# Each link between ScalarE and VectorE half a step later, in an encoder block with seven-product projections

## The chip, the cores and the metric

The kernel runs on one core of one Trainium2 chip. The time is the device time of an execution in microseconds. The core's engines are TensorE (PE in the profile: matmuls; PEld: its weight loads), VectorE (DVE), ScalarE (ACT), GpSimd (POOL) and SyncE (SP). Each has a queue that it works off strictly in the order in which the program issued, waiting on semaphores where an operand is not ready. DMAs are issued from SP, ACT or POOL.

## The reference

One layer of a hybrid encoder block on x (256 tokens, 2048 wide), all float32:

```python
xn = rms_norm(x, norm_pre_w)
u_lru, g_lru, q, k, v, g_attn, m_lru, m_attn = split(xn @ w_in)       # 2048 x 13312
u = centred_depthwise_conv(u_lru, conv_w, conv_b)
h = rg_lru(u, forward) + rg_lru(u, reverse)       # gates by 16 blocks of 128x128
y_a = h * silu(g_lru)
y_b = windowed_gqa(rope(q), rope(k), v, sink) * silu(g_attn)          # 16 heads, 4 kv heads
merged = sigmoid(m_lru) * (y_a @ w_proj_a) + sigmoid(m_attn) * (y_b @ w_proj_b)
out = x + rms_norm(merged @ w_out, norm_post_w)
```

## The kernel before

**Split products.** Every float32 operand is split into a high part (rounded to fp32r by a ScalarE cast) and a low part (what the cast left, by a VectorE subtraction). A product is then three fp32r matmuls: high by high, high by low, low by high (`mm3`, L226 to L228; in the wide form of a block, L249 and L250). So for each weight block ScalarE makes `wh` (L221) and VectorE makes `wl` (L223), both 128x1024 halves. `parts_of` (L152) does the same for activations: a cast (L153), then a subtraction (L154).

**Steps.** The program is a list of steps, each with a 1 MB block of weights; a step has two half-steps, each with 1024 columns of it. `load_plan` writes the order: 164 steps, 328 half-steps. A step is a "blk" (128 output columns in transposed form), a "quad" (a quarter of K for 512 columns, 12 matmuls of 512 in a half-step) or a "part" (one of the seven products, 6 matmuls of 512 in a half-step). The stages in order: u; the projections for the LRU branch and both SiLU gates (`gl`, `ga`, `u`); k and v; q with heads and the `ml` and `pa` products between; the merge gate of the attention branch (`ma`, `am`); four `pb` products; the output (`o`, `om`).

**The order within a half-step** is the loop at the end of `body`. At half-step hs it issues the loads (SP's queue; `fetch` with a lead of three steps, into three `raw` buffers), then everything registered for hs with `at` or `soon`, then `split(hs + 4)`, then what is registered `behind` hs, then the half-step's matmuls:

```python
for fn in due.pop(hs, ()):
    fn()
if hs >= FIRST:
    split(hs + 4)
```

So the cast of wh and the subtraction of wl stand next to each other in time, four half-steps ahead of their matmuls; there are five buffers for each. `soon(fn, d)` registers for d half-steps later. Within a function that is called at one half-step, a chain that goes from ScalarE to VectorE or back is issued whole: copy, add, scale, sigmoid, multiply in `silu_evac` and `scaled` (L523 to L528, L665, L666), reduce, exponentials in `expo`, cast and subtract in `parts_of`.

**Seven products.** Half of the merge gate (columns 512 to 1023 and so on, as named in `GATE`) and half of the output are computed in Strassen's manner: seven products of half size on sums of quarters, in place of eight. The sums of activations are made per 256 rows of K: `sums_of_parts` adds the parts of xs (`xx..a`, L319), `sums_of` makes four sums from it (`xx..f`, L311 to L313), and half a step later `parts_of` splits them into `xx`. Eight such calls are registered behind half-steps 3, 5, ... 17 of the gate. For the output the sums come from the transposed merged values (`turn`, L831; `mx`). The sums of weights are made by DMA: a cell (`amx0a` and so on: x or y, quarter 0 or 1, half a or b) is loaded, and after the product that used it, another block is added into it by a DMA from POOL's queue (L188). m5, m6 and m4 follow one another in the x cells, m7 follows m3 in the y cells. An add cannot be issued before the cell's wh and wl have been made. The order of the gate's 22 steps (a digit first is a quad of a plain column):

```python
GATE = "2.0 2.1 2.2 2.3 m1.0 m1.1 m2.0 m2.1 3.0 m5.0 m5.1 m3.0 m3.1 3.1 m6.0 m6.1 m7.0 m7.1 3.2 m4.0 m4.1 3.3".split()
```

The products are combined after m2, m6, m7 and m4 (`after`; VectorE, L382 to L388, then `combine`, L857), and the combination goes to ScalarE: a sigmoid in the gate (L676), squares in the output (L911).

Of the kernel before, what the change touches and what calls it, by code (L numbers as in the profile page):

```python
# [35 lines left out]
FIRST = 8  # L36
# [87 lines left out]
def body(ctx, tc, x, xT, wall, wlru, pvec, npost, ident_d, mask_d, rope_d, out):  # L124
    nc = tc.nc
# [16 lines left out]
    def half_unit(name, tag, dt=F32, bufs=2):  # L142
        return small.tile([P, 2, S], dt, tag=tag, name=name, bufs=bufs)
# [5 lines left out]
    def tiny(name, n=2):  # L149
        return small.tile([P, n], F32, tag="tiny", name=name, bufs=24)  # L150

    def parts_of(h, l, src, cast=nc.scalar.copy):  # L152
        cast(h, src)  # L153
        nc.vector.tensor_tensor(l, src, h.bitcast(F32), ALU.subtract)  # L154

# [19 lines left out]
    def soon(fn, d=1):  # L175
        at(now[0] + d, fn)
# [121 lines left out]

    SUMS = ("s3", "s1", "s2", "s4")

    def sums_of(name, src, psum=True):
        a = src.rearrange("p a b -> p (a b)")
        a11, a12, a21 = (a[:, i * P:(i + 1) * P] for i in (0, 2, 1))
        f = half_unit(f"{name}f", "uu", F32).rearrange("p a (b c) -> p (a b) c", b=2)
        t = unit(name, F32R, (P, 4, 2, P))
        ends = src.rearrange("p a (b c) -> p (a b) c", b=2)[:, 0:4:3]
        if psum:

            nc.scalar.copy(f[:, 3], a21)
            a21 = f[:, 3]  # L310
        nc.vector.tensor_tensor(f[:, 0:2], ends, a21.unsqueeze(1).to_broadcast([P, 2, P]), ALU.subtract)  # L311
        nc.vector.scalar_tensor_tensor(f[:, 2], f[:, 1], -1.0, a11, ALU.mult, ALU.subtract)
        nc.vector.scalar_tensor_tensor(f[:, 3], f[:, 2], -1.0, a12, ALU.mult, ALU.subtract)  # L313
        return t, f

    def sums_of_parts(name, pair, sums):

        a = half_unit(f"{name}a", "uu", F32)
        nc.vector.tensor_tensor(a, pair[:, :, 0].bitcast(F32), pair[:, :, 1].bitcast(F32), ALU.add)  # L319
        t, f = sums_of(name, a, False)  # L320
        sums.append(t)
        soon(lambda: parts_of(t[:, :, 0], t[:, :, 1], f))

    class Seven:

# [194 lines left out]
        upads[n] = t  # L520
        return t

    def scaled(dst, ps):  # L523
        if len(ps.shape) == 4:
            nc.scalar.copy(dst, ps[:, :, 1])
            nc.vector.tensor_tensor(dst, ps[:, :, 0], dst, ALU.add)
            ps = dst
        nc.vector.tensor_tensor(dst, ps, rbc.unsqueeze(1).to_broadcast([P, 2, S]), ALU.mult)  # L528

    def evac_quad(n):  # L530
        scaled(upad_tile(n)[:, :, 2:2 + S], ups[n // 2][:, :, 0])
# [126 lines left out]
    def silu_evac(units_list, n):  # L658
        def done(ps):
            if n % 4 == 0:  # L660
                units_list.append(unit(f"sg{n}"))
            dst = units_list[n // 4][:, n % 4:n % 4 + 2]
            sg = half_unit(f"sig{n}", "p")
            scaled(dst, ps)
            nc.scalar.activation(sg, dst, AF.Sigmoid)  # L665
            nc.vector.tensor_tensor(dst, dst, sg, ALU.mult)  # L666
        return done

    tm, sm, ms, msum = {}, {}, [], []
# [25 lines left out]
    def add_heads(name, then):  # L695

        v = {}

        def evac(n):
            def done(ps):  # L700
                v[n] = half_unit(f"{name}f{n}", "uu")
                scaled(v[n], ps)
                for d in range(4):
                    soon(lambda d=d: rotate(n, d), d + 1)
            return done

        def rotate(n, d):
            t = v[n]
            r = t[0:ROT]
            if d == 0:  # L710
                v["s"] = small.tile([ROT, 2, S], F32, tag="upad", name=f"{name}s{n}", bufs=2)
                nc.vector.stream_shuffle(v["s"], r, swap)
                nc.vector.tensor_tensor(r, r, rope[:, 0].unsqueeze(1).to_broadcast([ROT, 2, S]), ALU.mult)
            elif d == 1:
                s = v["s"]
                nc.vector.tensor_tensor(s, s, rope[:, 1].unsqueeze(1).to_broadcast([ROT, 2, S]), ALU.mult)
                nc.vector.tensor_tensor(r, r, s, ALU.add)
            elif d == 2:
                if n == 0:
                    v["h"], v["l"] = unit(f"{name}h", F32R), unit(f"{name}l", F32R)  # L720
                parts_of(v["h"][:, n:n + 2], v["l"][:, n:n + 2], t)
            elif n == 2:
                then(v["h"], v["l"])
                v.clear()

        for n in (0, 2):
            add_pair(f"{name}{n}", xs, evac(n))
# [4 lines left out]
    def v_evac(t, ps):  # L732
        if t == 0:
            kv["vh"], kv["vl"] = (unit(f"v{s}", F32R, (P, 2, 512)) for s in "hl")
        vh, vl = kv["vh"][:, t], kv["vl"][:, t]
        nc.scalar.activation(vh, ps, AF.Copy, scale=rtok[:, t:t + 1])
        nc.vector.scalar_tensor_tensor(vl, ps, rtok[:, t:t + 1], vh.bitcast(F32), ALU.mult, ALU.subtract)

    add_rows("v_ps", xs, v_evac)

    def head(hd, qh, ql, b):
        g, j = hd // 4, hd % 4
        sk = pv[:, PV_SINK + hd:PV_SINK + hd + 1]
        ts = [slice(t * P, (t + 1) * P) for t in range(2)]
        v = {}

        def scores():
            v["sc"] = bank(f"sc{hd}")
            for t in range(2):
                mm3(v["sc"][:, t], qh[:, j, ts[t]], ql[:, j, ts[t]], kv["kh"][:, g], kv["kl"][:, g], True, True)  # L750

        def expo():
            p = v["p"] = half_unit(f"p{hd}", "p")
            sc = v.pop("sc")
            m, nm, es = tiny(f"m{hd}"), tiny(f"nm{hd}"), tiny(f"es{hd}")
            dn = v["dn"] = tiny(f"dn{hd}")
            for t in range(2):
                nc.vector.tensor_tensor_reduce(p[:, t], sc[:, t], mask[:, t], P ** -0.5, sk, ALU.add, ALU.max, m[:, t:t + 1])
            nc.vector.tensor_scalar(nm, m, -1.0, None, ALU.mult)  # L759
            for t in range(2):  # L760
                nc.scalar.activation(p[:, t], p[:, t], AF.Exp, bias=nm[:, t:t + 1], accum_out=dn[:, t:t + 1])  # L761
            nc.scalar.activation(es, nm, AF.Exp, bias=sk)
            v["es"] = es

        def normalise():
            dn, rd = v["dn"], tiny(f"rd{hd}")
            nc.vector.tensor_tensor(dn, dn, v["es"], ALU.add)
            nc.vector.reciprocal(rd, dn)
            for t in range(2):
                nc.vector.tensor_scalar(v["p"][:, t], v["p"][:, t], rd[:, t:t + 1], None, ALU.mult)  # L770

        def flip():
            v["pt"] = bank(f"pt{hd}")
            for kt in range(2):
                for t in range(2):
                    nc.tensor.transpose(v["pt"][:, kt, ts[t]], v["p"][:, t, ts[kt]], ident)

        def p_parts():
            t = unit(f"ph{hd}", F32R, (P, 2, 2, S))
            v["h"], v["l"] = t[:, 0], t[:, 1]  # L780
            parts_of(v["h"], v["l"], v.pop("pt"))

        def values():
            v["o"] = bank(f"o{hd}")
            ks = slice(g * P, (g + 1) * P)
            for kt in range(2):
                mm3(v["o"][:, 0], kv["vh"][:, kt, ks], kv["vl"][:, kt, ks], v["h"][:, kt], v["l"][:, kt], kt == 0, kt == 1)

        def gate_out():
            y = sga[g][:, j]  # L790
            nc.vector.tensor_tensor(y, v["o"][:, 0], y, ALU.mult)
            v.clear()

        for d, fn in ((0, scores), (1, expo), (2, normalise), (4, flip), (5, p_parts), (7, values), (8, gate_out)):
            at(b + d, fn)

    def yb_parts(q):
# [18 lines left out]
    def add_pb(c):  # L816
# [8 lines left out]
        def turn(i):  # L825

            ps = bank(f"mt{c}{i}")
            for j in range(2):
                sl = slice((2 * i + j) * P, (2 * i + j + 1) * P)
                for t in range(2):  # L830
                    nc.tensor.transpose(ps[:, j, t * P:(t + 1) * P], sm[c][:, t, sl], ident)  # L831
            m = pair_unit(f"ms{2 * c + i}")
            ms.append(m)
            parts_of(m[:, :, 0], m[:, :, 1], ps)
            t, f = sums_of(f"mx{2 * c + i}", ps)
            parts_of(t[:, :, 0], t[:, :, 1], f)
            msum.append(t)

        add_rows(f"pb{c}_", yb, done)

# [14 lines left out]
    def combine(name, ps, other, sign):  # L855
        f = small.tile([P, 512], F32, tag="p", name=name, bufs=2)
        nc.vector.scalar_tensor_tensor(f, ps, float(sign), other, ALU.mult, ALU.add if sign > 0 else ALU.subtract)  # L857
        return f

    mid = []  # L860
    for m, c in MID:
        mid.append((add_pa, c // 512) if m == "w_proj_a" else (add_ml, (c - ML0) // 512))
# [5 lines left out]
        f(n)  # L868

    xsum = []  # L870
    seven = Seven("am", "w_in", MA0, xs, xsum, lambda t, c, ps, *a: gate_evac(sm, c)(t, combine(f"af{t}{c}", ps, *a)))
    b = 2 * len(steps)
    for q in range(2):
        at(b - 4 + 3 * q, lambda q=q, s=seven: s.start("x", q))
# [54 lines left out]
                eng = nc.sync if q % 2 == 0 else nc.scalar  # L929
                eng.dma_start(out[t * P:(t + 1) * P, q * 512:(q + 1) * 512], y)  # L930

    seven = Seven("om", "w_out", 0, ms, msum, lambda t, c, ps, *a: o_done(t, c, combine(f"of{t}{c}", ps, *a)))
    for q in range(2):
        at(b - 16 + 4 * q, lambda q=q, s=seven: s.start("x", q))
        at(b - 12 + 4 * q, lambda q=q, s=seven: s.second(q))
# [5 lines left out]
    for i, (_, half) in enumerate(steps):  # L941
        for h in range(2):
# [8 lines left out]
            for fn in due.pop(hs, ()):  # L951
                fn()
            if hs >= FIRST:
                split(hs + 4)
            if hs in last:
                last.pop(hs)()
            half(h, *parts.pop(hs))
# [72 lines left out]
```

## Time and profile before

| | |
|---|---|
| median of 3 runs | 926.21 us (924.91 to 926.62) |
| profiled execution, its own time | 925.56 us |
| its span, first to last instruction | 923.8 us |
| PE busy | 902.9 us (98%) |
| DVE busy | 716.5 us (78%) |
| ACT busy | 567.5 us (61%) |
| POOL busy | 29.4 us (3%) |
| HBM read | 186.10 MB, 204 GB/s over the span |
| granted TensorE clock, mean | 0.992 |

A row of a group or of a timeline has the line of the kernel, the engine, the operation, out<-in by the names in the program (buffer numbers left out), shapes, and the time; in brackets the idle time of that engine just before, and whose end ended it. In a timeline the first number is the start in us from the span's start and the second the time taken; "x2" merges neighbours. In the list of waits the numbers are us in total, times, and the longest. A PE matmul's time contains its drain, which overlaps the next one: starts, not durations, give the pace.

### The profile page before, as it was taken

Reading aid. Unit: us, or ns where it says so; the run is one execution under the profiler, and the core shown is the slowest. Engines: PE = TensorE matmul, PEld = TensorE weight load, DVE = VectorE, ACT = ScalarE, POOL = GpSimd, SP = SyncE. Lnnn points to the kernel's source line nnn. Section 1 sums busy time; section 2 is a strip of 40 time slices with the busy share of each in tenths; the row PEclk is TensorE's granted clock in tenths of the full one; section 3 lists DMA queues with packets and bytes.
Section 4 is the critical chain, followed back from the end, with each engine's and each line's share of the span. In section 5 each row is a group of like instructions: output and inputs, shape, how many; then the busy total and the mean of one; then the engine's idle time right before and its main releaser. Section 6 shows DMA issues by size and latency. Waiting matters only on the chain.

```text
span 923.8 us, 12335 instructions
## 1 busy us (share of the span) xinstructions
PE 902.9 (98%) x4742; PEld 769.7 (83%) x4742; DVE 716.5 (78%) x1010; ACT 567.5 (61%) x794; POOL 29.4 (3%) x55
## 2 busy tenths in 40 slices
PE   9999999999999999999999999999978999999996
PEld 8898888888888888888888888888756788888885
DVE  6976968696979889896877878556677867778786
ACT  7678585858497875955554454644446654445653
POOL 0000000000000000000000000001003000100210
PEclk9999999999999999999999999999989999999999
DMA  9765455446455454466445444559769674987992
GB/s 339 264 216 193 158 203 201 168 155 230 154 205 205 157 186 169 154 224 228 144 176 182 148 172 140 180 186 292 258 203 191 146 259 176 302 293 280 231 317 102
DMA packets 33372, 189.00 MB, mean 205 GB/s; under 512 B 3712, under 2 KB 4480, under 8 KB 15264
## 3 DMA queue, kind: packets, MB, share of 16 engines
q1 hardware_dynamic: 27840, 170.14, 51.5%
q0 software_dynamic: 4608, 16.78, 9.6%
q10 hardware_dynamic: 864, 1.29, 0.4%
q8 instruction: 37, 0.61, 0.3%
q14 instruction: 23, 0.19, 0.1%
HBM read 186.10 MB, written 2.10 MB: 204 GB/s over the span
## 4 chain that ended last, share of the span: by engine, by line
PE 86%; issue 7%; DMA 3%; POOL 1%; DVE 1%; ACT 0%; SPq 0%; DVEq 0%; ACTq 0%; POOLq 0%
PE ga L250 6%; PE q L250 6%; PE gl L250 6%; PE u L250 5%; PE ga L249 3%; PE q L249 3%; PE gl L249 3%; PE u L249 2%; PE u_ps L509 2%; PE k L250 2%; PE omm L226 1%; PE omm L227 1%; PE omm L228 1%; DMA amx1b<-wall_dram 1%; PE o L228 1%
## 5 line engine op out<-in xcount | busy, mean ns | idle before, releaser
L223 DVE TENSOR_TENSOR wl<-raw,wh 128x1024 fp32r<-128x1024 f32 (+1 forms) x290 | 348.1, 1213 | 130.8 <-ACT wh L221 129.9
L221 ACT CAST wh<-raw 128x1024 fp32r<-128x1024 f32 (+1 forms) x289 | 296.1, 1043 | 122.1 <-PE q L250 14.4
L250 PE MATMUL ga<-xs,wh 128*128 128x512 f32 x256 | 90.6, 398 | 0.0
L250 PE MATMUL q<-xs,wh 128*128 128x512 f32 x256 | 89.8, 396 | 0.0
L250 PE MATMUL gl<-xs,wh 128*128 128x512 f32 x224 | 79.3, 398 | 0.0
L250 PE MATMUL u<-xs,wh 128*128 128x512 f32 x192 | 68.0, 398 | 0.0
L249 PE MATMUL ga<-xs,wl 128*128 128x256 f32 x240 | 67.5, 281 | 0.0
L249 PE MATMUL q<-xs,wl 128*128 128x256 f32 x240 | 67.1, 280 | 0.0
L249 PE MATMUL gl<-xs,wl 128*128 128x256 f32 x210 | 59.0, 281 | 0.0
L250 PEld LDWEIGHTS ga<-xs,wh 128*128 128x128 f32 x256 | 47.6, 188 | 10.4
L250 PEld LDWEIGHTS q<-xs,wh 128*128 128x128 f32 x256 | 47.4, 188 | 9.9
L249 PE MATMUL u<-xs,wl 128*128 128x256 f32 x180 | 50.6, 281 | 0.0
L250 PEld LDWEIGHTS gl<-xs,wh 128*128 128x128 f32 x224 | 41.7, 188 | 9.1
L249 PEld LDWEIGHTS ga<-xs,wl 128*128 128x128 f32 x240 | 45.4, 189 | 0.6
L249 PEld LDWEIGHTS q<-xs,wl 128*128 128x128 f32 x240 | 45.3, 189 | 0.7
L250 PEld LDWEIGHTS u<-xs,wh 128*128 128x128 f32 x192 | 35.7, 188 | 7.8
L249 PEld LDWEIGHTS gl<-xs,wl 128*128 128x128 f32 x210 | 39.7, 189 | 0.6
L761 ACT ACTIVATE p<-p,nm 128x256 f32<-128x256 f32 x32 | 16.0, 502 | 37.9 <-DVE nm L759 37.9
L249 PEld LDWEIGHTS u<-xs,wl 128*128 128x128 f32 x180 | 34.0, 189 | 0.5
L665 ACT ACTIVATE sig<-sg 128x512 f32<-128x512 f32 x16 | 10.1, 632 | 34.2 <-DVE sg L528 34.2
L585 DVE SCALAR_TENSOR_TENSOR uu<-upad,pv,uu 128x256 f32<-128x256 f32 x48 | 23.3, 485 | 2.3
L250 PE MATMUL k<-xs,wh 128*128 128x512 f32 x64 | 22.5, 398 | 0.0
(525 smaller groups left out, 2230.7 us busy)
## 6 DMA issues: line engine op xcount, KB each, us to landing
raw<-wall_dram SPq DMA_DIRECT2D x141, 1024.0 KB, 4.8
lraw<-wlru_dram SPq DMA_DIRECT2D x8, 512.0 KB, 5.6
raw<-wall_dram SPq DMA_DIRECT2D x4, 512.0 KB, 7.0
xr<-x_dram SPq DMA_DIRECT2D x4, 512.0 KB, 12.8
amx0a<-wall_dram POOLq DMA_DIRECT2D x3, 512.0 KB, 9.3
amx0b<-wall_dram POOLq DMA_DIRECT2D x3, 512.0 KB, 8.4
amx1a<-wall_dram POOLq DMA_DIRECT2D x3, 512.0 KB, 7.5
amx1b<-wall_dram POOLq DMA_DIRECT2D x3, 512.0 KB, 7.5
```

What stands on the lines that cost most here:

```text
L221: cast(hs, raw)
L223: nc.vector.tensor_tensor(ls, raw, hs.bitcast(F32), ALU.subtract)
L226: nc.tensor.matmul(ps, wh, xh, start=start, stop=False)
L227: nc.tensor.matmul(ps, wh, xl, start=False, stop=False)
L228: nc.tensor.matmul(ps, wl, xh, start=False, stop=stop)
L249: nc.tensor.matmul(ps[:, 1], wl[:, sl], a[:, 0], start=False, stop=False)
L250: nc.tensor.matmul(ps, wh[:, sl], a, start=k == 0, stop=k == KT - 1)
L509: nc.tensor.matmul(ups[b // 2][:, b % 2, 0], w[:, sl], a[:, m], start=k == 0 and n == 0, stop=k == KT - 1 and n == 2)
L585: nc.vector.scalar_tensor_tensor(u, up[:, j, tap:tap + S], cw[:, tap:tap + 1], u, ALU.mult, ALU.add)
L665: nc.scalar.activation(sg, dst, AF.Sigmoid)
L761: nc.scalar.activation(p[:, t], p[:, t], AF.Exp, bias=nm[:, t:t + 1], accum_out=dn[:, t:t + 1])
```

## The change

Where ScalarE and VectorE feed one another, the next link is registered with `soon` for the next half-step and no longer issued at once:

- `parts_of`: the cast now, the subtraction one half-step later.
- The main loop: wh of hs + 4 and wl of hs + 3 at half-step hs. From the eighth half-step on; the first are as before.
- `scaled`: the copy now, add and scale a half-step later; in `silu_evac` the sigmoid another one later, the multiply one after that.
- `sums_of`: with a PSUM source, the copy now and the sums a half-step later; their cast one later, the subtraction another one later. Without, the sums now, and so on.
- `v_evac`: the low part of v a half-step later. `expo`: the exponentials a half-step after the maxima.
- The products of the gate and of the output: sigmoid or squares a half-step after the combination.
- Fixed distances move with it: `rotate` by one half-step; of a head, `normalise`, `flip`, `p_parts` by one, `values` and `gate_out` by two.

```diff
-    def parts_of(h, l, src, cast=nc.scalar.copy):
-        cast(h, src)
-        nc.vector.tensor_tensor(l, src, h.bitcast(F32), ALU.subtract)
+    def parts_of(h, l, src):
+        nc.scalar.copy(h, src)
+        soon(lambda: nc.vector.tensor_tensor(l, src, h.bitcast(F32), ALU.subtract))
...
-    def sums_of(name, src, psum=True):
+    def sums_of(name, src, sums, psum):
...
+        def make(a21):
+            nc.vector.tensor_tensor(f[:, 0:2], ends, a21.unsqueeze(1).to_broadcast([P, 2, P]), ALU.subtract)
+            nc.vector.scalar_tensor_tensor(f[:, 2], f[:, 1], -1.0, a11, ALU.mult, ALU.subtract)
+            nc.vector.scalar_tensor_tensor(f[:, 3], f[:, 2], -1.0, a12, ALU.mult, ALU.subtract)
+            soon(lambda: parts_of(t[:, :, 0], t[:, :, 1], f))
+
         if psum:
             nc.scalar.copy(f[:, 3], a21)
-            a21 = f[:, 3]
...
+            soon(lambda: make(f[:, 3]))
+        else:
+            make(a21)
...
-    def scaled(dst, ps):
+    def scaled(dst, ps, then=lambda: None):
+        def scale(src):
+            nc.vector.tensor_tensor(dst, src, rbc.unsqueeze(1).to_broadcast([P, 2, S]), ALU.mult)
+            then()
+
+        def total():
+            nc.vector.tensor_tensor(dst, ps[:, :, 0], dst, ALU.add)
+            scale(dst)
+
         if len(ps.shape) == 4:
             nc.scalar.copy(dst, ps[:, :, 1])
-            nc.vector.tensor_tensor(dst, ps[:, :, 0], dst, ALU.add)
-            ps = dst
-        nc.vector.tensor_tensor(dst, ps, rbc.unsqueeze(1).to_broadcast([P, 2, S]), ALU.mult)
+            soon(total)
+        else:
+            scale(ps)
...
-            scaled(dst, ps)
-            nc.scalar.activation(sg, dst, AF.Sigmoid)
-            nc.vector.tensor_tensor(dst, dst, sg, ALU.mult)
+
+            def sigmoid():
+                sg = half_unit(f"sig{n}", "p")
+                nc.scalar.activation(sg, dst, AF.Sigmoid)
+                soon(lambda: nc.vector.tensor_tensor(dst, dst, sg, ALU.mult))
+
+            scaled(dst, ps, lambda: soon(sigmoid))
...
-                    soon(lambda d=d: rotate(n, d), d + 1)
+                    soon(lambda d=d: rotate(n, d), d + 2)
...
-        for d, fn in ((0, scores), (1, expo), (2, normalise), (4, flip), (5, p_parts), (7, values), (8, gate_out)):
+        for d, fn in ((0, scores), (1, expo), (3, normalise), (5, flip), (6, p_parts), (9, values), (10, gate_out)):
...
+    def then(fn, t, f):
+        soon(lambda: fn(t, f))
+
...
-    seven = Seven("am", "w_in", MA0, xs, xsum, lambda t, c, ps, *a: gate_evac(sm, c)(t, combine(f"af{t}{c}", ps, *a)))
+    seven = Seven("am", "w_in", MA0, xs, xsum, lambda t, c, ps, *a: then(gate_evac(sm, c), t, combine(f"af{t}{c}", ps, *a)))
...
             if hs >= FIRST:
-                split(hs + 4)
+                split(hs + 4, only="h")
+                if hs > FIRST:
+                    split(hs + 3, only="l")
```

More of the change, by code (lines that the diff above doesn't have):

```diff
@@ L299, in body @@
     SUMS = ("s3", "s1", "s2", "s4")
-    def sums_of(name, src, psum=True):
+    def sums_of(name, src, sums, psum):
         a = src.rearrange("p a b -> p (a b)")
         a11, a12, a21 = (a[:, i * P:(i + 1) * P] for i in (0, 2, 1))
+        ends = src.rearrange("p a (b c) -> p (a b) c", b=2)[:, 0:4:3]
         f = half_unit(f"{name}f", "uu", F32).rearrange("p a (b c) -> p (a b) c", b=2)
         t = unit(name, F32R, (P, 4, 2, P))
-        ends = src.rearrange("p a (b c) -> p (a b) c", b=2)[:, 0:4:3]
+        sums.append(t)
+        def make(a21):
[3 more added lines that the diff above has]
+            soon(lambda: parts_of(t[:, :, 0], t[:, :, 1], f))
         if psum:
             nc.scalar.copy(f[:, 3], a21)
-            a21 = f[:, 3]
[L311 to L314, printed above, removed]
+            soon(lambda: make(f[:, 3]))
+        else:
+            make(a21)
     def sums_of_parts(name, pair, sums):
@@ L319, in sums_of_parts @@
         nc.vector.tensor_tensor(a, pair[:, :, 0].bitcast(F32), pair[:, :, 1].bitcast(F32), ALU.add)
-        t, f = sums_of(name, a, False)
-        sums.append(t)
-        soon(lambda: parts_of(t[:, :, 0], t[:, :, 1], f))
+        sums_of(name, a, sums, False)
     class Seven:
@@ L662, in done @@
             dst = units_list[n // 4][:, n % 4:n % 4 + 2]
-            sg = half_unit(f"sig{n}", "p")
-            scaled(dst, ps)
-            nc.scalar.activation(sg, dst, AF.Sigmoid)
-            nc.vector.tensor_tensor(dst, dst, sg, ALU.mult)
+            def sigmoid():
[3 more added lines that the diff above has]
+            scaled(dst, ps, lambda: soon(sigmoid))
         return done
@@ L736, in v_evac @@
         nc.scalar.activation(vh, ps, AF.Copy, scale=rtok[:, t:t + 1])
-        nc.vector.scalar_tensor_tensor(vl, ps, rtok[:, t:t + 1], vh.bitcast(F32), ALU.mult, ALU.subtract)
+        soon(lambda: nc.vector.scalar_tensor_tensor(vl, ps, rtok[:, t:t + 1], vh.bitcast(F32), ALU.mult, ALU.subtract))
     add_rows("v_ps", xs, v_evac)
@@ L759, in expo, with exps @@
             nc.vector.tensor_scalar(nm, m, -1.0, None, ALU.mult)
+            soon(lambda: exps(p, nm, es, dn))
+        def exps(p, nm, es, dn):
             for t in range(2):
@@ L834, in turn @@
             parts_of(m[:, :, 0], m[:, :, 1], ps)
-            t, f = sums_of(f"mx{2 * c + i}", ps)
-            parts_of(t[:, :, 0], t[:, :, 1], f)
-            msum.append(t)
+            sums_of(f"mx{2 * c + i}", ps, msum, True)
         add_rows(f"pb{c}_", yb, done)
@@ L930, in o_done @@
                 eng.dma_start(out[t * P:(t + 1) * P, q * 512:(q + 1) * 512], y)
-    seven = Seven("om", "w_out", 0, ms, msum, lambda t, c, ps, *a: o_done(t, c, combine(f"of{t}{c}", ps, *a)))
+    seven = Seven("om", "w_out", 0, ms, msum, lambda t, c, ps, *a: then(lambda t, f: o_done(t, c, f), t, combine(f"of{t}{c}", ps, *a)))
     for q in range(2):
```

## The prediction

> **What bounds the kernel now.** I read the stretches first (busy time per engine), then what TensorE waits for, then the instructions of VectorE and ScalarE in time order where it waits. Five stretches; columns are PE, weight loads, DVE, ACT, POOL busy with instruction counts, then granted clock, DMA share, GB/s:
>
> ```profile
> 0.00:15.00 15.00, 13.04 (x88) 12.32 (x89) 8.11 (x15) 8.95 (x15) 0.61 (x11) 1.00 0.86 301
> 15.00:662.40 647.40, 647.40 (x3618) 563.07 (x3617) 512.10 (x756) 417.41 (x602) 4.45 (x16) 1.00 0.55 192
> 662.40:742.70 80.30, 68.78 (x265) 51.91 (x264) 61.54 (x78) 45.69 (x54) 10.42 (x12) 0.94 0.75 194
> 742.70:905.00 162.30, 162.28 (x728) 133.36 (x727) 122.30 (x144) 89.45 (x112) 13.94 (x16) 1.00 0.83 260
> 905.00:924.00 19.00, 11.38 (x51) 9.05 (x49) 12.48 (x21) 5.95 (x12) 0.00 (x0) 0.88 0.30 111
> ```
>
> TensorE is full from 15 to 662 and from 743 to 905: there, VectorE's and ScalarE's waits cost nothing, and nothing can be won. Only the gate stage (662 to 743) has room. How much follows from the pace of a 512-wide matmul when nothing waits:
>
> ```profile
> 383.65 0.39 PE L228 MATMUL v_ps<-wh,xs 128*128 128x512 f32 x1
> 384.79 0.39 PE L227 MATMUL v_ps<-wl,xs 128*128 128x512 f32 x1
> 385.92 0.39 PE L226 MATMUL v_ps<-wh,xs 128*128 128x512 f32 x1
> ```
>
> Ten matmuls start in 2.27 us, so 0.227 each. The stage's 264 need 59.9 us and take 80.3: **20.4 us are lost**. Half-steps below are counted from the gate's first (0 to 43; the row of 662.40 starts with half-step 8): a half-step of a seven-products part is 6 matmuls or 1.36 us, one of a quad 12 or 2.72 us. The losses, by what TensorE waited for:
>
> ```profile
> PE amm L226 <- ACT wh L221: 3.5, 3, 1.7
> PE amm L227 <- DVE wl L223: 3.0, 4, 0.8
> PE ma__6341 L226 <- ACT wh L221: 2.1, 1, 2.1
> PE amm L226 <- ACT xx L153: 1.4, 1, 1.4
> ```
>
> 10.0 us are waits for split weights or sums, no more than 2.1 at a time. A granted clock of 0.94 over 80.3 us is another 4.8 us of withheld pulses; the rest is draining and refilling around the stalls. So the stage is bound by the loop of ScalarE and VectorE that makes wh, wl and the sums. One turn of it (one sum, two half-steps) on VectorE:
>
> ```profile
> 668.41 2.36 DVE L223 TENSOR_TENSOR wl<-raw,wh 128x1024 fp32r<-128x1024 f32 x2 [2.82 <-ACT wh L221]
> 670.69 0.68 DVE L319 TENSOR_TENSOR xx3a<-xs 128x512 f32<-128x512 f32 x1
> ...
> 673.17 0.69 DVE L154 TENSOR_TENSOR xx<-xx3f,xx 128x512 fp32r<-128x512 f32 x1 [0.68 <-ACT xx L153]
> 674.11 2.36 DVE L223 TENSOR_TENSOR wl<-raw,wh 128x1024 fp32r<-128x1024 f32 x2 [0.26 <-ACT wh L221]
> ```
>
> The turn takes 674.11 - 668.41 = 5.70 us, of it 0.94 waiting and about 4.75 work. TensorE wants it in 2.72 us (parts) or 5.44 (quads). Over all eight sums, in the stretch from 650.6 to 700.7:
>
> ```profile
> DVE wl L223 <- ACT wh L221: 6.6, 8, 2.8
> DVE xx L154 <- ACT xx L153: 5.5, 8, 0.7
> ```
>
> **The change on the bounding loop.** The low part of a sum and the wl of a weight now stand one half-step behind the ScalarE cast that feeds them. VectorE's order becomes: sum, wl, low part, wl, next sum. While ScalarE casts the sum (0.62 us), VectorE does a wl (1.14 us back to back); the next wh is cast meanwhile. Both kinds of wait, 12.1 us, have other VectorE work under them, except where ScalarE itself is late:
>
> ```profile
> 664.88 1.28 ACT L676 ACT_TABLE_LOAD   x1
> 666.18 1.27 ACT L676 ACTIVATE mg<-ma__6019,rtok 128x512 f32<-128x512 f32 x2
> 667.33 1.99 ACT L221 CAST wh<-raw 128x1024 fp32r<-128x1024 f32 x2
> ```
>
> The sigmoids of ma__6019 must follow TensorE's half-step 7 (about 662.5), so the cast of half-step 12's wh is ready near 664.8, while VectorE arrives near 662.5: 2.3 us of wait stay. With 0.4 for the m1 copy ahead of a cast, 2.7 remain of the 12.1. VectorE's anchors:
>
> ```profile
> 646.64 1.23 DVE L223 TENSOR_TENSOR wl<-raw,wh 128x1024 fp32r<-128x1024 f32 x1 [1.38 <-ACT wh L221]
> ...
> 650.46 0.68 DVE L319 TENSOR_TENSOR xx0a<-xs 128x512 f32<-128x512 f32 x1
> ...
> 699.50 1.23 DVE L223 TENSOR_TENSOR wl<-amy0a,wh 128x1024 fp32r<-128x1024 f32 x1 [0.26 <-ACT wh L221]
> ```
>
> Before, from the first sum (650.46) to the end of wl of half-step 22 (700.73) are 50.3 us, 38.2 of them work. After, the first sum follows the wl of half-step 6, which ends at 647.87, not that of 7. To the work come that wl (1.14) and the low part of the last head's probabilities (0.6), which drifts in: 39.9, plus 2.7 of wait gives **690.5 in place of 700.73: 10.2 us**. Bounds: 7 if as much again stays waited for, 12.6 if nothing is.
>
> From there TensorE sets the pace:
>
> ```profile
> 700.78 0.75 PE L227 MATMUL amm<-wl,xx 128*128 128x512 f32 x1 [0.75 <-DVE wl L223]
> ...
> 742.73 0.39 PE L226 MATMUL pb__6751<-wh,yb 128*128 128x512 f32 x1
> ```
>
> Those 41.95 us hold 167 matmuls, 37.9 us at full pace: 4.05 lost. The sigmoids of the combined products, now a half-step behind the combination, no longer hold the casts on ScalarE, which removes these losses. But the weights of these products are added up by DMAs on POOL's queue:
>
> ```profile
> 687.61 0.87 POOL L188 DMA_DIRECT2D amx0a<-wall_dram  x1 [46.07 <-DVE wl L223]
> ...
> 701.13 0.87 POOL L188 DMA_DIRECT2D amy0a<-wall_dram  x1 [3.68 <-DVE wl L223]
> ...
> 706.85 0.88 POOL L188 DMA_DIRECT2D amy1b<-wall_dram  x1 [1.76 <-DVE wl L223]
> 710.20 0.87 POOL L188 DMA_DIRECT2D amx0a<-wall_dram  x1 [2.47 <-issue]
> ...
> 718.38 0.86 POOL L188 DMA_DIRECT2D amx1a<-wall_dram  x1 [2.90 <-issue]
> 720.84 0.87 POOL L188 DMA_DIRECT2D amx1b<-wall_dram  x1 [1.61 <-DVE wl L223]
> ```
>
> ```profile
> amx0a<-wall_dram POOLq DMA_DIRECT2D x3, 512.0 KB, 9.3
> ...
> amx1b<-wall_dram POOLq DMA_DIRECT2D x3, 512.0 KB, 7.5
> amy0a<-wall_dram POOLq DMA_DIRECT2D x1, 512.0 KB, 5.4
> ...
> amy1b<-wall_dram POOLq DMA_DIRECT2D x1, 512.0 KB, 11.2
> ```
>
> An add goes out just after the third one before it has landed: y0a lands at 706.5 and y1b leaves at 706.85; y1b lands at 718.05 and x1a leaves at 718.38. So three are in flight. After the change the first add follows the wl of half-step 18, two turns and a combination (0.65) before 690.5: it leaves near 680.8. The wl ends behind it are 684.1, 685.8, 688.8 and 690.5. With landings of 7.5 to 9.3 us the fourth add waits for the first (lands 690.1), y0a for the second (692.8) and leaves at 693.1, and y1b waits for y0a (693.1 + 5.4) and leaves at 699.4, to land at 710.6. Cast and wl make 713.0; TensorE wants it at 710.9 (half-step 22 starts one matmul ahead of 690.5, at 690.3; 90 matmuls to half-step 35 are 20.4, and its first runs on wh). **2.1 us of stall**, bounds 0 and 6. The last add lands near 719.6, ready at 722.0, wanted at 723.9: no stall.
>
> One cost of the clock stays open, since TensorE will still stop for 1 to 1.6 us at a time around half-steps 15 to 21. The 4.8 us of withheld pulses fell in about two spells; one more spell costs 0 (it falls where TensorE waits anyway) to 2.4. I take 0.8, nearer to nothing, as the stops are shorter. The Trainium skill, page "TensorE: Matmul & The Clock Gate", section "What's actually happening", lets the clock halve after an idle window of about 3.4 us; by it the term would be 0 and the time 914.1. The trace disagrees: clock was withheld although no wait here exceeds 2.1 us.
>
> **The change elsewhere.** Every half-step leaves TensorE a lead of three for wl, not four. Least room is in the v projection:
>
> ```profile
> 381.65 0.67 DVE L716 TENSOR_TENSOR ks<-ks,rope 32x512 f32<-32x512 f32 x1
> ...
> 382.97 1.21 DVE L223 TENSOR_TENSOR wl<-raw,wh 128x1024 fp32r<-128x1024 f32 x1
> ```
>
> That wl ends at 384.18 for the matmul of 384.79 quoted above: 0.6 us of room. If a rotation of 1.32 us comes ahead of it, 0.7 us is lost; its cover is that VectorE no longer waits for casts ahead of it. Cost 0, bounds 0 and 2. The load of each weight block waits for a wl that is now half a step later:
>
> ```profile
> raw<-wall_dram SPq DMA_DIRECT2D x141, 1024.0 KB, 4.8
> ```
>
> It still has four half-steps (10.9 us in quads) until its cast, less about 3 us of VectorE work, against 4.8 us: cost 0. Heads run three half-steps later, so the last head's product moves from gate half-step 4 to 7; its consumers start at 36. The evacuations hold their PSUM a half-step longer, with two more half-steps until it is wanted. Instructions are the same ones, but for table loads that ScalarE's new order may add or save; off the gate ScalarE has room. In the tail the last products are evacuated directly: 0.
>
> **Sum.** 10.2 + 4.05 - 2.1 - 0.8 = 11.3 us off the profiled execution's 925.56 (span 923.8 and 1.8 around it): 914.2. The median of the runs is 926.21, 0.65 above it: **914.9 us**, 911 to 918.5 by the terms' bounds.
>
> **Rivals.** *The adds decide.* If the adds keep their spacing (687.61 to 720.84, 33.2 us) and only the first is earlier by 6.8, the stage ends 6.8 us earlier: 919.4. For it: three in flight, and more traffic in less time. Against it: part of that spacing was VectorE's lateness. The skill's page "SBUF — State Buffer", section "Who interferes with whom", has VectorE with two SBUF inputs contend with GpSimd reads, which would delay adds under a denser VectorE; the issues' 0.86 to 0.88 us beside running subtractions show no such thing. *All stalls go*: 20.4 off, 905.8. Against it: 39.9 us of VectorE work still exceed TensorE's demand. *Nothing moves*: the waits pass to ScalarE, whose cast of a sum now stands ahead of wh and waits for VectorE; 926. Against it: that wh is wanted four half-steps later. *Slower*: the wl of an added cell comes a half-step later behind other work, so each of the three adds in turn (m5 to m6, m3 to m7, m6 to m4) leaves up to 2.72 us later, 8.2 in all. The last landed before at about 728.4 (720.84 and 7.5), ready at 730.8, wanted at 735.9 (742.73 less the 30 matmuls from there): 5.1 us of room, so 3.1 are lost, 929.3. It decides only if wl of half-step 18 ends later than 687.25; with waits gone I get 680.4.
>
> **How the numbers follow.** Forecast 0.58, adds 0.20, all stalls gone 0.06, nothing 0.09, slower 0.07. A measurement of this kernel tells 0.2% (1.9 us). Faster 0.84, same 0.09, slower 0.07. The range 908.5 to 921.5 takes in the adds' case with 2 us of spread and the forecast with the larger bound of VectorE's term and no stall.
>
> **What would show it.** In the profile after: low parts of sums and wl in the gate without waits but one of about 2 us; the wl of the first y cell ending near 690 rather than 700.73; first add near 681; pb starting near 731; TensorE's waits in the stage under 6 us and clock at or above 0.97; TensorE still full from 15 to 660. Wrong: TensorE waits in the v projection or the output stage, adds spaced as before, or VectorE waiting as much on other names.

## The result, and the profile after

The changed kernel takes **913.71 us** (median of 4 runs, 913.40 to 914.34), the kernel before 925.63 beside it (4 runs, 924.91 to 926.62). The ratio is 0.9871, with a 95% interval of 0.9854 to 0.9888: faster by 1.3%. The forecast was 914.9, within 908.5 to 921.5. The profiled execution took 914.34 us with a span of 912.6, so 11.2 us of span are gone.

The stretches after the change (columns as in the prediction: busy time of PE, weight loads, DVE, ACT and POOL, then granted clock, DMA share, GB/s):

```profile
15.00:662.40 647.40, 647.40 (x3615) 563.50 (x3614) 513.49 (x760) 416.84 (x599) 4.46 (x16) 1.00 0.55 192
662.40:731.00 68.60, 63.15 (x266) 48.70 (x266) 58.26 (x74) 45.81 (x56) 10.46 (x12) 1.00 0.85 224
731.00:893.00 162.00, 161.98 (x728) 133.06 (x727) 120.21 (x144) 89.28 (x111) 13.97 (x16) 1.00 0.84 262
```

TensorE is as full as before outside the gate stage. Within it 266 matmuls lie in 68.6 us, where 265 took 80.3 before, and the granted clock is 1.00 where it was 0.94. The whole difference arises there: the first product after the stage starts at

```profile
731.60 0.39 PE L228 MATMUL pb__6750<-wh,yb 128*128 128x512 f32 x1
```

instead of 742.73, which is 11.1 us earlier. What TensorE waits for in the gate, and the one turn of VectorE that answers to the one shown of before (a turn is one sum and two half-steps):

```profile
PE amm L229 <- DVE wl L225: 4.6, 4, 1.5
PE ma__6337 L229 <- DVE wl L225: 0.6, 1, 0.6
```

```profile
666.71 0.68 DVE L326 TENSOR_TENSOR xx3a<-xs 128x512 f32<-128x512 f32 x1
...
668.21 0.29 DVE L314 SCALAR_TENSOR_TENSOR xx3f<-xx3f,xx3a 128x128 f32<-128x128 f32 x1
668.42 1.22 DVE L225 TENSOR_TENSOR wl<-raw,wh 128x1024 fp32r<-128x1024 f32 x1
669.56 0.69 DVE L156 TENSOR_TENSOR xx<-xx3f,xx 128x512 fp32r<-128x512 f32 x1
670.16 1.22 DVE L225 TENSOR_TENSOR wl<-raw,wh 128x1024 fp32r<-128x1024 f32 x1
671.29 0.68 DVE L326 TENSOR_TENSOR xx4a<-xs 128x512 f32<-128x512 f32 x1
```

The waits for wh and xx are gone, and 5.2 us of waits are left of 11.2: to the 10.0 of the prediction's four rows comes one more row of the kernel before:

```profile
PE ma__6341 L227 <- DVE wl L223: 1.2, 2, 0.8
```

The turn runs from 666.71 to 671.29, 4.58 us with no bracket in it, in place of 5.70 with 0.94 of waiting. VectorE is now busy through the turn. ScalarE still waits for the sums, but for less: 2.1 us at each of five of them and at most 0.3 at the other three, where it was 3.0 to 3.2 at each of the eight. Further on it now waits for the added weights. First one cast of a sum before, then the changed kernel:

```profile
678.23 0.62 ACT L153 CAST xx<-xx4f 128x512 fp32r<-128x512 f32 x1 [3.19 <-DVE xx4f L313]
```

```profile
673.13 0.62 ACT L155 CAST xx<-xx4f 128x512 fp32r<-128x512 f32 x1 [2.06 <-DVE xx4f L314]
...
710.36 1.05 ACT L223 CAST wh<-amy1b 128x1024 fp32r<-128x1024 f32 x1 [1.42 <-DMA amy1b<-wall_dram]
...
722.15 1.05 ACT L223 CAST wh<-amx1b 128x1024 fp32r<-128x1024 f32 x1 [2.12 <-DMA amx1b<-wall_dram]
```

### The profile page after: what moved, and what is told of

It is laid out like the page before. It is cut to its first block, busy times and chain, and to the rows that moved or that the text cites. A ratio compares the mean times of both kernels' runs of the same rounds, so it can differ in the third digit from the quotient of the medians.

```text
span 912.6 us, 12347 instructions
## 1 busy us (share of the span) xinstructions
PE 898.3 (98%) x4742; PEld 767.9 (84%) x4742; DVE 712.0 (78%) x1010; ACT 566.1 (62%) x789; POOL 29.5 (3%) x55
## 4 chain that ended last, share of the span: by engine, by line
PE 87%; issue 6%; DMA 5%; DVE 1%; POOL 1%; ACT 0%; SPq 0%; DVEq 0%; ACTq 0%; POOLq 0%
PE ga L252 7%; PE q L252 7%; PE gl L252 6%; PE u L252 5%; PE ga L251 3%; PE q L251 3%; PE gl L251 3%; DMA amx1b<-wall_dram 2%; PE u L251 2%; PE u_ps L514 2%; PE k L252 2%; PE omm L229 1%; PE omm L230 1%; PE omm L228 1%; DMA amy1a<-wall_dram 1%
## 5 line engine op out<-in xcount | busy, mean ns | idle before, releaser
L223 ACT CAST wh<-raw 128x1024 fp32r<-128x1024 f32 (+1 forms) x289 | 300.4, 1045 | 226.1 <-PE q L252 37.9
L252 PEld LDWEIGHTS ga<-xs,wh 128*128 128x128 f32 x256 | 47.6, 188 | 10.4
L774 DVE CUSTOM_DVE_ANT_0 p<-sc,mask,pv 128x256 f32<-128x256 f32 x32 | 14.2, 478 | 9.2 <-PE sc L230 8.9
L680 DVE TENSOR_TENSOR sg<-sg,sig 128x512 f32<-128x512 f32 x16 | 11.0, 689 | 10.4 <-ACT sig L679 10.3
```

The lines of the kernel that those rows point to most:

```text
L223: cast(hs, raw)
L252: nc.tensor.matmul(ps, wh[:, sl], a, start=k == 0, stop=k == KT - 1)
L680: soon(lambda: nc.vector.tensor_tensor(dst, dst, sg, ALU.mult))
```

## The experiments

Those named together stand beside the same runs of the kernel before: e1 to e4 beside a median of 925.12 us, e5 to e8 beside 925.49, e9 to e12 beside 925.12.

**Which links carry the gain (e1, e2).** e1 moves the kinds of link that lie on the gate's path: wl, `parts_of`, the sums, and the step after a combination. It moves them wherever the kernel has them, so in the output stage too. e2 moves the others alone: `scaled`, SiLU, rotations, v and the heads.

```diff
+    def parts_of(h, l, src):
+        nc.scalar.copy(h, src)
+        soon(lambda: nc.vector.tensor_tensor(l, src, h.bitcast(F32), ALU.subtract))
...
-                split(hs + 4)
+                split(hs + 4, only="h")
+                if hs > FIRST:
+                    split(hs + 3, only="l")
```

> Only the links that the gate stage uses are moved (wl, low parts, sums, sigmoid after a combination); the SiLU chains, the head chains, the exponentials and the low part of v are as before. Theory (the gain is VectorE's waits in the gate stage alone): as the changed kernel, 913.7 us within 1. Rival (links elsewhere give part of it by shortening TensorE's stream or by the lead): about half of the gain, 919 us.

```diff
-                    soon(lambda d=d: rotate(n, d), d + 1)
+                    soon(lambda d=d: rotate(n, d), d + 2)
...
+            soon(lambda: exps(p, nm, es, dn))
```

> The complement: only the SiLU chains, the head chains, the exponentials and the low part of v are moved. Theory: TensorE is full there, so nothing, 925.6 us within 1. Rival: about 919 us.

e1 took 913.75 us (ratio 0.9873, 0.9850 to 0.9896), e2 925.28 (0.9997, 0.9985 to 1.0009). The gain is in the links of e1, and the rest costs and brings nothing, as the full TensorE from 15 to 662 says.

**wl alone, and the sums alone (e3, e4).** e3 is the kernel before with wl at hs + 3. e4 is the kernel before with only the low part of a sum half a step behind its cast.

```diff
-                split(hs + 4)
+                split(hs + 4, only="h")
+                if hs > FIRST:
+                    split(hs + 3, only="l")
```

> The kernel before with wl alone a half-step later. Theory: the 8 waits of the sums' low parts (5.5 us) stay and the waits of wl go; wl of half-step 22 near 696 in place of 690.8, the sigmoid behind the combination still holds the casts: 919 to 921 us. Rival (the wl waits alone set the stage): 914 us.

```diff
-        soon(lambda: parts_of(t[:, :, 0], t[:, :, 1], f))
+        def cast():
+            nc.scalar.copy(t[:, :, 0], f)
+            soon(lambda: nc.vector.tensor_tensor(t[:, :, 1], f, t[:, :, 0].bitcast(F32), ALU.subtract))
+
+        soon(cast)
```

> The kernel before with the low part of the gate's sums alone a half-step later; wl still directly behind its cast. Theory: the wait does not go, it passes to wl, which must now sit through the cast of the sum and that of wh (1.6 us) without the low part's 0.6 us as cover; a turn of 6.3 us in place of 5.7, 8 turns: 4 to 5 us slower, 928 to 930 us. Rival (each link taken apart gives its own wait back, 5.5 us): 920 us.

e3 took 920.23 us (ratio 0.9938, 0.9918 to 0.9958), e4 **929.25 (1.0043, 1.0032 to 1.0054)**: four tenths of the gain, and a loss. (e3's gate ends earlier by more than that, 6.8 of 11.1 us with pb at 735.93, but its output stage takes 1.6 us longer than before.) VectorE's waits from 650.6 to 702, first of e3, then of e4:

```profile
DVE xx L154 <- ACT xx L153: 5.6, 8, 0.8
DVE wl L223 <- ACT wh L221: 2.6, 3, 1.7
```

```profile
DVE wl L223 <- ACT wh L221: 16.0, 8, 4.2
```

Before, they were 5.5 for sums and 6.6 for wh. e3 leaves the eight waits for sums as they were and takes 4.0 us off those for wh. e4 takes away all the waits for sums, and the waits for wh grow from 6.6 to 16.0. Why is seen in one turn of e4, first on ScalarE, then on VectorE:

```profile
680.59 0.62 ACT L323 CAST xx<-xx4f 128x512 fp32r<-128x512 f32 x1 [3.79 <-DVE xx4f L313]
681.11 0.58 ACT L380 COPY amc<-amm 128x512 f32<-128x512 f32 x1
681.59 1.99 ACT L221 CAST wh<-raw 128x1024 fp32r<-128x1024 f32 x2
```

```profile
680.26 0.29 DVE L313 SCALAR_TENSOR_TENSOR xx4f<-xx4f,xx4a 128x128 f32<-128x128 f32 x1
682.67 1.22 DVE L223 TENSOR_TENSOR wl<-raw,wh 128x1024 fp32r<-128x1024 f32 x1 [2.11 <-ACT wh L221]
```

ScalarE waits at the cast of the sum, and the cast of wh is queued behind it. VectorE, after the sum, has nothing but the wl of this wh next, so it waits for both casts. Before, it waited for the one and, after the low part, for the rest of the other. That is the mechanism of the rival "nothing moves" (waits pass to ScalarE), and it does hold when wl isn't moved too. With both moved, a wl of the half-step before stands between, and VectorE has work while ScalarE casts the sum.

**The sigmoid after a combination (e5).** The kernel before with the edits of e3 and e4 together: the sigmoid after the combination, the squares of the output and the output's sums stay whole.

> The kernel before, with two links moved: wl of the weights, and the low parts of the gate's sums. The sigmoid after the combination and all other links stand as before. Theory T (the gain comes from wl and the sums together, and the later sigmoid of the combination is worth little, since the cast queued behind it is wanted only four half-steps later): 914.0 us, 913 to 915, the first product of the output projection starting near 731 us. Rival R (the combination's sigmoid, which held casts in ScalarE's queue, carries a good part of the 4 us that the prediction gave to the time after half-step 22): 915 to 917, with waits of VectorE of 1 us or more behind that sigmoid.

It took **916.85 us** (0.9907, 0.9892 to 0.9922). That is the rival's time, but not for the rival's reason, and T was right on the gate (731 us) and wrong on the time: the gate ended as early as in the changed kernel, and 2.5 us of span were lost later.

```profile
731.62 0.39 PE L226 MATMUL pb__6750<-wh,yb 128*128 128x512 f32 x1
...
835.55 0.50 PE L227 MATMUL o__7430<-wl,ms 128*128 128x512 f32 x1 [0.93 <-DVE wl L223]
...
900.82 0.50 PE L227 MATMUL o<-wl,ms 128*128 128x512 f32 x1 [0.98 <-DVE wl L223]
```

TensorE stops twice in the output stage; by the starts of the matmuls, each stop costs 1.25 us. The first comes behind the output's sums, still in whole chains, which hold VectorE (in e5):

```profile
831.92 0.42 DVE L311 TENSOR_TENSOR mx7f<-mt,mx7f 128x256 f32<-128x256 f32 x1 [0.33 <-ACT mx7f L309]
...
833.67 0.69 DVE L154 TENSOR_TENSOR mx<-mx7f,mx 128x512 fp32r<-128x512 f32 x1 [0.69 <-ACT mx L153]
834.28 5.76 DVE L223 TENSOR_TENSOR wl<-raw,wh 128x1024 fp32r<-128x1024 f32 x5
```

The second comes behind the last combination and the output's steps after it, which in e5 stand ahead of the wl of 899.55. e1, which moves the output's links too, has neither stop. So the shorter lead of wl is free only because those links were moved with it. The sigmoid itself is worth nothing in the gate, within the 0.5 us by which the profiles of e1 and of the changed kernel differ at pb.

**The lead itself (e8).** The changed kernel with wl at hs + 2.

```diff
-                if hs > FIRST:
-                    split(hs + 3, only="l")
+                if hs > FIRST + 1:
+                    split(hs + 2, only="l")
```

> The changed kernel, with wl of half-step hs + 2 made at half-step hs, in place of hs + 3: its lead over TensorE is one half-step shorter again, all else stands. Theory T (the lead of three is no more than what is needed in places: the least room behind a wl outside the gate is 0.11 us in the output projection, below 1 us at four half-steps there): TensorE waits there and in the gate, 915 to 919 us. Rival R (VectorE has so much room that a lead of two costs nothing): 913.7 us within 1.

It took 918.26 us (0.9930, 0.9909 to 0.9952), some 4.6 more than the changed kernel, and T holds on the time. Two of the stops that its profile adds:

```profile
50.16 0.50 PE L229 MATMUL ml<-wl,xs 128*128 128x512 f32 x1 [0.40 <-DVE wl L225]
...
863.24 0.50 PE L229 MATMUL omm<-wl,mx 128*128 128x512 f32 x1 [1.13 <-DVE wl L225]
```

The gate hardly changed (pb starts at 731.86): T was wrong on the place there. Of the leads tried (four, three, two), three is the shortest that is free.

**What holds the gate now (e6, e7, e9, e11, e12, with e10).** e6 doubles the scratch in which POOL's DMAs keep their descriptors. e7 puts the sigmoids of the plain ma columns half a step later. e9 does both. e11 is e7 with six buffers of wh and four of wl in place of five and five; e12 is e11 with the scratch. e10 is the changed kernel once more.

```diff
-    add_mixed(seven, GATE, lambda c: add_rows(f"ma{c}_", xs, gate_evac(sm, c)))
+    add_mixed(seven, GATE, lambda c: add_rows(f"ma{c}_", xs, lambda t, ps: then(gate_evac(sm, c), t, ps)))
...
-    nc = bacc.Bacc("TRN2", target_bir_lowering=False, num_devices=1, dynamic_dma_scratch_size=1024)
+    nc = bacc.Bacc("TRN2", target_bir_lowering=False, num_devices=1, dynamic_dma_scratch_size=2048)
...
-            parts[q] = [ring.tile([P, 1024], F32R, tag=f"w{s}", name=f"w{s}{i}_{h}", bufs=5) for s in "hl"]
+            parts[q] = [ring.tile([P, 1024], F32R, tag=f"w{s}", name=f"w{s}{i}_{h}", bufs=6 if s == "h" else 4) for s in "hl"]
```

> The changed kernel, with twice the scratch for the descriptors of POOL's DMAs and nothing else. Theory T (what holds the add of y1b until 699.87 us, 9 us behind the end of the first y cell's wl, is that only three of these adds fit in the scratch at once): the adds leave as soon as their wl is written, that of y1b near 695 us, the stalls of some 2.1 us at half-steps 34 to 36 and of 0.5 us at the last add go: 911.5 us, 910.5 to 912.5. Rival R (the DMA engines' throughput sets when the adds land): they leave earlier and land as late, 913.7 us within 0.8.

> The changed kernel, with the sigmoids of the plain ma columns in the gate one half-step later in ScalarE's queue as well. Theory T (VectorE's one wait of 2.3 us that is left, behind the table load and these sigmoids, makes the whole chain of adds later by as much): the wait goes, wl of half-step 22 is written near 688.5 us instead of 690.80, the time is 911.4 us, 910.5 to 912.5. Rival R (the adds hold the stage, not VectorE's turns): that wl may end earlier, but the adds land within 0.7 us of where they did and the time is 913.7 us within 0.8.

> The changed kernel with the larger scratch for POOL's DMAs and with the sigmoids of the plain ma columns a half-step later. Theory T (the larger scratch is worth the 1.4 us by which its output projection began earlier in the profile, and VectorE's 0.3 us from the later sigmoids adds to it): 912.0 us, 911.4 to 912.6. Rival R (from 690 to 720 us the DMA engines are full, share 1.04 and 1.05, and what is issued earlier lands as late): 913.3 us within 0.6, as the unchanged one beside it.

> The changed kernel as it is, beside the three that follow on the same chip, so that they can be set against it directly: 913.5 us, 912.9 to 914.3.

> The changed kernel with the later sigmoids and with six buffers of wh and four of wl in place of five and five, so that ScalarE's cast needn't wait until TensorE has ended the half-step before. Theory T (VectorE's wait of 1.17 us that the later sigmoids left goes too, wl of half-step 22 is written near 688.7 us, and the adds follow it): 911.8 us, 911.0 to 912.6. Rival R (the wl is that early, but the DMA engines are full and the adds land within 0.7 us of where they did): 913.3 us within 0.6. Rival S (four buffers tie VectorE to TensorE's half-step before last elsewhere): 914.5 or more, with waits of TensorE for wl outside the gate.

> The same as the one before, with the larger scratch for POOL's DMAs as well. Theory T (VectorE and the limit of three held the stage together): 910.5 us, 909.8 to 911.3. Rival R (the DMA engines' throughput holds it): 913.0 us within 0.7, the last product of the gate, m4, waiting for its added weights as before.

| | median us (4 runs) | wl of half-step 22 ends, us after fourth half-step | pb starts, us after it |
|---|---|---|---|
| changed kernel | 913.71 (913.40 to 914.34) | 675.1 | 715.9 |
| the same, e10 | 913.54 (913.23 to 914.21) | 675.1 | 714.8 |
| e6, scratch | 913.30 (912.93 to 914.22) | 675.1 | 714.6 |
| e7, sigmoids later | 913.22 (913.02 to 914.33) | 674.7 | 715.8 |
| e9, both | 913.50 (912.92 to 913.67) | 674.7 | 714.3 |
| e11, buffers | 913.15 (912.46 to 913.48) | 674.5 | 714.5 |
| e12, buffers, scratch | 912.52 (912.11 to 912.82) | 674.5 | 714.6 |

The last two columns are from the profiles, counted from the start of TensorE's fourth half-step, which lies anywhere from 14.7 to 16.6 us. The same kernel twice (rows 1 and 2) differs by 1.1 us at pb, so the last column tells no row but perhaps e9 from the second. In the middle column these two agree within 0.1.

*e7 and e11: T fell.* VectorE's wait of 2.28 us was expected to go whole. It shrank to 1.17, and another of 0.58 came:

```profile
664.56 1.23 DVE L225 TENSOR_TENSOR wl<-raw,wh 128x1024 fp32r<-128x1024 f32 x1 [1.17 <-ACT wh L223]
...
668.07 1.23 DVE L225 TENSOR_TENSOR wl<-raw,wh 128x1024 fp32r<-128x1024 f32 x1 [0.58 <-ACT wh L223]
```

because in e7 the cast ahead of it has its own wait, for a wh buffer that TensorE still reads:

```profile
663.47 1.05 ACT L223 CAST wh<-raw 128x1024 fp32r<-128x1024 f32 x1 [1.50 <-PE ma__6005 L230]
```

With six buffers of wh (e11) the cast is early, and VectorE waits for one of its four wl buffers instead, up to the first y cell:

```profile
DVE wl L225 <- PE ma__6005 L229: 2.3, 3, 1.5
```

So 4.5 us of waits in VectorE's term became 3.9 in e7 and 3.7 in e11, and the wl of half-step 22 came 0.4 and 0.6 us earlier.

*e6: the limit is there, and isn't what binds.* The adds of the last y cells, first in the changed kernel, then in e6:

```profile
695.77 0.86 POOL L190 DMA_DIRECT2D amy1a<-wall_dram  x1 [1.77 <-DVE wl L225]
699.87 0.88 POOL L190 DMA_DIRECT2D amy1b<-wall_dram  x1 [3.23 <-issue]
```

```profile
693.31 0.86 POOL L190 DMA_DIRECT2D amy1a<-wall_dram  x1 [0.27 <-issue]
694.45 0.86 POOL L190 DMA_DIRECT2D amy1b<-wall_dram  x1 [0.27 <-issue]
```

With the scratch doubled they leave one after the other. But the add of y1b leaves 5.4 us earlier and takes 14.6 us instead of 10.4, so it lands 1.2 us earlier; of the 2.1 us of stall at half-steps 34 to 36, 0.8 are left in this profile. The DMA engines are full in that stretch, in the changed kernel (first) as in e6 (second):

```profile
690.00:705.00 15.00, 14.93 (x66) 12.02 (x65) 13.03 (x12) 10.39 (x11) 4.72 (x6) 1.00 1.04 217
705.00:720.00 15.00, 13.48 (x58) 10.47 (x58) 11.46 (x14) 9.38 (x11) 2.60 (x3) 1.00 1.05 235
```

```profile
690.00:705.00 15.00, 14.92 (x66) 11.97 (x65) 13.01 (x12) 10.29 (x11) 7.11 (x9) 1.00 1.05 221
705.00:720.00 15.00, 14.51 (x64) 11.72 (x63) 12.83 (x15) 9.33 (x11) 0.00 (x0) 1.00 1.05 241
```

The share is 1.04 to 1.05, the most that any stretch shown has, at 217 to 241 GB/s. That is R's mechanism, and the times of e6 and e9 are R's; so are those of e7, e11 and e12. e12 lies 1.0 us under e10 with no run in common, the fastest of all, but 0.1% is under what four runs tell here, and its profile doesn't place it: beside e9 and e11 its gate is no shorter.

## Why the prediction was right

**The loop of VectorE and ScalarE bounds the stage.** Right: e1 has all of the gain, e2 none.

**Both kinds of wait go.** Right, and only together (e3, e4, e5). VectorE's waits for sums are gone, and those for wh fell to the ones in which ScalarE is late. The wl of the first y cell:

```profile
689.58 1.22 DVE L225 TENSOR_TENSOR wl<-amy0a,wh 128x1024 fp32r<-128x1024 f32 x1
```

It ends at 690.80; 690.5 was forecast. The term is 9.9 us for 10.2. Its parts were off and made up for one another: the first sum began at 647.34 (forecast 647.87), the work was 39.0 us (39.9), and the waits were 4.5 (2.7). The 1.8 missed are two waits in the quads ahead of half-step 8, of 1.03 and 0.76 us, in which the cast has to wait for TensorE to free a wh buffer. The prediction had counted only the sigmoids and the m1 copy. That the sum came within 0.3 us is in part luck.

**The time after half-step 22.** Forecast: 4.05 off, 2.1 of stall and 0.8 of clock back, 1.15 net. Measured: from the end of that wl to pb, 42.0 us (742.73 less 700.73) became 40.8 (731.60 less 690.80), 1.2 net. The stall at half-steps 34 to 36 is 4.86 us for what takes 2.72 at full pace: 2.1, as forecast. Its chain of adds was right to the microsecond: first add 681.38 (forecast 680.8), y1b leaves 699.87 (699.4), wl of y1b ends 713.38 (713.0). It is not all the add's: the wh of y1b, quoted above, is ready at 711.41, but VectorE is in a combination until 712.16, so 0.75 is VectorE's order.

```profile
710.11 0.68 DVE L387 TENSOR_TENSOR amu<-amm,amc 128x512 f32<-128x512 f32 x1
...
712.16 1.22 DVE L225 TENSOR_TENSOR wl<-amy1b,wh 128x1024 fp32r<-128x1024 f32 x1
```

Two sizes were off and cancelled. The last add was to land at 719.6 without a stall; its cast waited for it until 722.15, and half-steps 41 and 42 lost 0.6. The clock was to cost 0.8 and cost nothing.

**The sentence that failed** is the reason given for the 4.05: "The sigmoids of the combined products ... no longer hold the casts on ScalarE, which removes these losses". By the starts of the matmuls, 1.7 of the 4.05 us went while the clock was at half, where those sigmoids have no part (in the kernel before; the third column from the end is the granted clock):

```profile
700.86:704.27 3.41, 3.41 (x8) 2.69 (x9) 3.41 (x4) 3.39 (x4) 1.78 (x3) 0.50 1.01 178
```

Another 2.2 went in stops, 1.4 from 723.9 on and 0.8 from 733.9 on, where casts did stand behind a sigmoid. After the change the clock is full, and the stops cost 2.1 and 0.6 us: others, around the added weights, have taken the place of those that went. So the net gain there is the clock's 1.7 us, less what the stops grew by, and the forecast met it by luck. e5 leaves those sigmoids where they were, and its pb starts at 731.62; from its wl of half-step 22 (ends at 690.55) to pb are 41.1 us. e3, with wl alone, has 40.9 (695.00 to 735.93). e2, which moves neither but whose clock is full in that stretch, has 41.3 (700.10 to 741.38). What the output's later links bring shows in e5's two stops in the output stage, and the prediction had it at zero.

**Elsewhere 0.** Right in time. That it rests on the output's own links was not seen: the prediction looked for the least room in the v projection, where the room grew. It is now least behind the squares of the output:

```profile
861.05 0.69 DVE L936 TENSOR_TENSOR yw<-o__7430,np 128x512 f32<-128x512 f32 x1 [0.75 <-ACT junk L931]
861.66 1.22 DVE L225 TENSOR_TENSOR wl<-omx0b,wh 128x1024 fp32r<-128x1024 f32 x1
...
863.00 0.44 PE L229 MATMUL omm<-wl,mx 128*128 128x512 f32 x1
```

That wl ends at 862.88 and is read from 863.00 on: 0.1 us.

**The sum.** 914.2 was forecast for the profiled execution, and it took 914.34, the slowest of its four runs; that closeness is luck. The 0.65 us added for the median of before was scatter: beside the other runs, the kernel before had medians of 925.63, 925.12 and 925.49. *The adds decide* (919.4) was right on the adds and wrong on the end: they kept nearly their spacing (681.38 to 713.02 is 31.6 us, before 33.2), but the stage ended 11.1 us earlier and not 6.8, since the last add had some 5 us of room before, which is now used up. The issues of the adds took 0.86 to 0.88 us as before, beside a denser VectorE. *Slower* fell by the condition it named: the wl of half-step 18 ended well before 687.25, at 681.03:

```profile
679.81 1.22 DVE L225 TENSOR_TENSOR wl<-amx0a,wh 128x1024 fp32r<-128x1024 f32 x1
```

## What to carry to other kernels

Where two engines feed each other through queues worked off in order, a consumer placed right behind its producer in program order pays the producer's time in each turn, though neither engine is full; the cure is to have other work of the waiting engine between the two. It has to be done for every link of the loop: a single link moved can win a part (e3), or put the remaining ones behind one another and lose (e4). Before a lead is shortened to pay for it, look for the least room over the whole kernel, and behind chains that stay whole above all (e5, e8).

## What was not expected of the hardware

The clock. In the stage the granted clock was 0.94 before and in e2, 0.90 in e4, but 1.00 in e3 and in the changed kernel. The length of a single wait of TensorE doesn't order them: the longest is 2.1 us before, 3.7 in e2, 2.4 in e4, 2.6 in e3 and 1.5 after.

In these profiles the clock is at 1.00 or at 0.50. It is at 0.50 for 3.41 us or a multiple, and in each run the changes lie on one grid of 3.41 us: before, from 680.38 to 687.21 and from 700.86 to 704.27, and then, 63 such windows later, from 919.32 at the end of the run. So TensorE's busy time can be read window by window (length, then PE busy; in e3 the grid is counted back from 914.62, its only change). First two windows of the kernel before, then two of e4, then two of e3:

```profile
676.97:680.38 3.41, 1.28 (x7) 0.74 (x5) 1.88 (x6) 2.15 (x4) 0.00 (x0) 1.00 0.82 274
680.38:683.79 3.41, 2.93 (x6) 2.04 (x7) 3.34 (x5) 0.84 (x1) 0.00 (x0) 0.50 0.17 46
```

```profile
694.96:698.38 3.42, 1.62 (x6) 1.13 (x7) 2.40 (x3) 1.94 (x3) 0.82 (x1) 1.00 0.90 170
698.38:701.79 3.41, 2.27 (x6) 1.10 (x5) 2.18 (x5) 1.10 (x2) 0.93 (x2) 0.50 0.79 126
```

```profile
685.93:689.35 3.42, 1.83 (x8) 1.05 (x6) 2.83 (x4) 2.61 (x3) 0.86 (x1) 1.00 0.83 163
689.35:692.76 3.41, 1.87 (x7) 1.05 (x6) 2.62 (x7) 1.37 (x2) 0.86 (x1) 1.00 0.89 139
```

TensorE is idle for 2.13 us of the first window and for 1.80 of the third, and half clock follows; it is idle for 1.59 us of the fifth, and the clock stays full. In all 14 profiles together, from 20 us on, 21 windows at full clock are followed by one at half, each with 1.80 us idle or more, and no window followed by full clock has more than 1.59. So it is the sum of the stops within a window that counts, and the limit here lies between 1.59 and 1.80 us of 3.41 (idle by the profile's ends of matmuls, which are modelled). Where the windows' edges fall counts too, and they fall differently in each run: e3's wait of 2.6 us lies across the edge at 692.76. Its full clock is in part luck. The changed kernel has at most 1.49 us idle in a window of the gate.

The Trainium skill, page "TensorE: Matmul & The Clock Gate", section "What's actually happening", has the clock follow how busy TensorE was in a window of about 3.4 us that runs freely. The traces agree with the window, by the 3.41 us above; that a window must be idle as a whole, as the prediction took it, they don't bear out.

The adds. Twelve of 0.5 MB keep the DMA engines full from 690 to 720 us beside the loads of weights (share 1.04 and 1.05), and the one add followed here, sent 5.4 us earlier into that, took 4.2 us longer (14.6 for 10.4).
